# A hybrid decoder layer: DMA issues of recurrence and attention in source order, rotary products behind the exchange, low-rank chain begun later

## The chip, the cores and the metric

The kernel runs on 1 core of one Trainium2 chip. The metric is the device time of one execution in microseconds (us), lower is better. The core has five engines with their own instruction streams: TensorE (PE, matmul; its weight loads are shown as PEld), VectorE (DVE), ScalarE (ACT), GpSimd (POOL) and SyncE (SP). In this kernel SP issues all DMA transfers. Each engine takes its instructions strictly in the order of its stream, and an instruction that waits for a semaphore holds up those behind it.

## The reference, cut to what matters

One decoder layer on 1024 tokens of width 1024, all in float32. A gated merge of two mixers is followed by an MLP and a gated embedding:

```
u = rmsnorm(h);  z = u @ w_in
o_attn = dilated_attention(z_attn)        # 3 groups, (window, dilation) = (128,1), (512,4), (2048,16); 4 heads of 64 each
o_rwkv = rwkv7_time_mix(z_rwkv, ...)      # 8 heads of 64, a recurrence over the tokens
merged = sigmoid(z_gate_a) * (o_attn @ w_attn_up) + sigmoid(z_gate_r) * (o_rwkv @ w_rwkv_up)
h = h + rmsnorm(merged @ w_out)
h = h + rmsnorm(square(relu(rmsnorm(h) @ w_ff_in)) @ w_ff_out)
h = h + rmsnorm((p @ w_ple) * sigmoid(h @ w_ple_gate))
```

Queries and keys of the attention are rotated before the scores (rotary embedding): `rope(x) = [x1*cos - x2*sin, x2*cos + x1*sin]`, with x1 and x2 the two halves of a head. The recurrence needs a decay, a learning rate and a gate for each token and channel; these come from three low-rank products, for example `decay = exp(-exp(-softplus(-(w0 + tanh(xw) @ w2)) - 0.5))`.

## The kernel before

**Precision.** Every large product is made of three single-pass matmuls over high and low halves (`mm3`: high x high, high x low, low x high; lines 284, 286 and 288). A weight tile therefore needs two products before use: ACT writes the high half `wh`, POOL the low half `wl = wr - wh`.

**Stages.** First x is normalised and transposed into `uh` and `ul`, while the first two column tiles of z (inputs of the low-rank chain) are multiplied. Then come recurrence and attention, the part that the change touches. The output projection, the FFN and the embedding follow.

**Dense jobs.** The 46 further column tiles of z are dense jobs on PE: 12 for the recurrence (r, k, v for each of four pairs of heads, `add_rkv`), 18 for the attention (q, k, v for each of six pairs of heads, `add_attn`) and 16 for the gates (`add_gate`). A job has 2 halves of 24 matmuls. Each half is evacuated by ACT, and a gate's half is stored to DRAM (`gscr`). When a job begins, `fill` draws the next one and calls its `load`; `wload` (line 305) issues the DMA of 512 KB into one of two raw buffers `wr` and has the split on ACT and POOL emitted 3.9 us later in the plan (`soon(HOP_DMA + 1.4, split)`), or at the latest when that job begins. The very first job's split is therefore emitted as soon as it is drawn.

**Chains.** Everything else runs as Python generators beside the dense jobs: `lora_out` (the low-rank products, 24 stores to DRAM), `prepare` with `elementwise(w)` and `bonus(w)`, `inverses`, `rwkv` (`fold_v`, `fold`, `scan`, `read_out`, `post`) and `attention` (`turn`, `unit`). In `unit`, each block of 128 queries goes through scores on PE (`sc`), maximum on DVE (`SB`, `nm`), exponential on ACT, transposition on PE (`pt`), a copy on DVE (`PB`) and the product with V on PE (`po`).

**Who sets the order.** `Order` (line 131) is a planner that runs at build time. It keeps a modelled clock `t` for PE and an end for each engine, and lets each chain go on when its time has come; chains of lower priority number first, and a dense job's next matmul when no chain is due. The order in which instructions are emitted is the source order. Engines in a `manual_schedule` set keep this order: PE in the whole kernel (line 248), DVE, ACT and POOL from line 1167 to the end of `combine` (line 1161 leaves it). Before the change SP is in no such set: the framework's scheduler orders its DMA issues at build time by a model of its own, and may bring an issue forward as soon as its buffer and data are free. `spawn(gen, prio, after)` adds a chain that is first due `after` us from now. `HOP_DMA` is 2.5 us, the planner's price of a DMA from issue to landing. A POOL product is priced at 0.15 us and 0.0022 us for each element of a row.

**Rotary.** When the second half of a q or k tile `z` has been evacuated, four DMAs copy it with the halves of each head exchanged into `sw` (line 935). DVE multiplies `z` by the cosine in place (line 936). The chain `turned` (line 917) is due 2.7 us later: POOL multiplies `sw` by the sine, and after POOL's planned end DVE adds both.

**Elementwise and bonus.** `elementwise(w)` takes the tiles `En` and `a` (one buffer each) and loads the low-rank results into them. `bonus(w)` multiplies in the same buffer `a` and stores it to `bvscr`, after `elementwise(w)` has finished. Before the change, `elementwise(w + 1)` could take `a` in the source ahead of that store.

Of the kernel before, what the change touches and what calls it, by code (L numbers as in the profile page):

```python
# [13 lines left out]
OP = mybir.AluOpType  # L14
# [21 lines left out]
HOP, HOP_DMA = 0.15, 2.5  # L36
# [201 lines left out]
def layer(ctx: ExitStack, tc: tile.TileContext, x, pT, wz, wup, w_out, wff1, w_ff2, w_ple, w_pleg,  # L238
# [3 lines left out]
    sch = Order()  # L242
    SY = Loads(nc.sync, sch)
    V = Engine(nc.vector, sch, 0.18, 0.00104, True)
# [19 lines left out]
    done = set()  # L264

    def mm(out_, a, b, us, start=True, stop=True):
        PE.matmul(out_, a, b, start=start, stop=stop)  # L267
        m = math.prod(a.shape[1:])
        sch.turn("full" if a.shape[0] > 64 and m > 64 else (a.shape[0], m))
        sch.t = max(sch.t, sch.written.since(a, None) - 0.1, sch.written.since(b, None) - 0.1) + us  # L270
        sch.written.put(out_, sch.t, None)
        sch.dep = sch.t
# [8 lines left out]
    def mm3(ps, pairs):  # L281
        n = len(pairs)
        for i, (ah, al, bh, bl) in enumerate(pairs):
            PE.matmul(ps, ah, bh, start=i == 0, stop=False)  # L284
            yield MM
            PE.matmul(ps, ah, bl, start=False, stop=False)  # L286
            yield MM
            PE.matmul(ps, al, bh, start=False, stop=i == n - 1)  # L288
            yield MM

    def now(gen):
        for us in gen:
            sch.t += us
            sch.dep = sch.t

    def wait(cond):
        while not cond():
            yield 0.1

    def chain_bank(shape, name, tags=("m0", "m1")):  # L300
        tag = sch.first(tags)
        yield from sch.free(tag)
        return psum.tile(shape, F32, name=name, tag=tag), tag
# [134 lines left out]
    def rtile(shape, name, tag, dt=F32):  # L438
        n = 1
        for d in shape[1:]:  # L440
            n *= d
        assert n <= TAGN[tag], (shape, tag)
        return rt.tile(shape, dt, name=name, tag=tag, bufs=BUFS.get(tag, 1))
# [20 lines left out]
    def add_z(wi, evac, gate=None):  # L464
        def body(hi, lo):
            for h in range(2):
                ps = zbank()
                yield from zhalf(ps, hi, lo, h)
                evac(h, ps)
        sch.add(body, lambda: wload(wz[wi]), gate)  # L470
# [39 lines left out]
    def lora_out():  # L510
        S.activation(xw[0:96], xw[0:96], AF.Tanh)
        S.activation(xwh[0:96], xw[0:96], AF.Copy)
        V.tensor_tensor(xwh[32:64], xw[32:64], xwh[32:64], OP.subtract)
        S.activation(xg[0:96], xg[0:96], AF.Sigmoid)
        S.activation(xgh[0:96], xg[0:96], AF.Copy)
        V.tensor_tensor(xgl[0:96], xg[0:96], xgh[0:96], OP.subtract)
        S.activation(xa3[0:96], xar[0:96], AF.Copy)
        V.tensor_tensor(xa3[32:64], xar[32:64], xa3[32:64], OP.subtract)
        yield 9.0
        i = 0  # L520
        for w, n in [(w, n) for n in range(3) for w in range(NU)]:
            sl = slice(w * 128, w * 128 + 128)
            dst = (sa_scr[2 * w], sa_scr[2 * w + 1], og_scr[w])[n]
            for h in range(2):
                hs = slice(h * 512, h * 512 + 512)
                ps, tag = yield from chain_bank([128, 512], "lo", ("m0", "m1", "s1", "s2", "s3"))
                if n == 0:
                    mm(ps, wsh[0:96, sl], xwh[0:96, hs], MM)
                elif n == 1:
                    mm(ps, a2h[0:96, sl], xa3[0:96, hs], MM)  # L530
                else:
                    now(mm3(ps, [(g2r[0:96, 0, sl], g2r[0:96, 1, sl], xgh[0:96, hs], xgl[0:96, hs])]))
                st = lst[:, i % 8]
                i += 1
                if n < 2:
                    bc = (P_W0, P_A0)[n] + w
                    S.activation(st, ps, AF.Sigmoid, bias=pr[:, bc:bc + 1])
                else:
                    S.activation(st, ps, AF.Copy)
                sch.hold(tag)  # L540
                SY.dma_start(dst[:, hs], st)
                yield 0.6
            done.add(("lo", n, w))
# [32 lines left out]
    XY = {}  # L576

    def elementwise(w):
        yield from wait(lambda: ("lo", 1, w) in done)
        pc = lambda c: pr[:, c + w:c + w + 1]  # L580
        En = rtile([128, T], "En", "En")
        Ep = rtile([128, T], "Ep", "Ep")
# [292 lines left out]
    def prepare():  # L875
        for w in range(NU):
            yield from wait(lambda: w < 2 or ("F", w - 2) in done)
            yield from elementwise(w)
# [8 lines left out]
    def rwkv():  # L887
        for w in range(NU):
            yield from fold_v(w)
            yield from wait(lambda: ("T", w) in done)  # L890
            yield from fold(w)
            yield from scan(w)
            yield from read_out(w)
# [3 lines left out]
    rope_t, MD, NAT = {}, {}, {}  # L897

    def attn_ok(n, x):
        if n < 2:  # L900
            return (("S", NU - 2) in done and ("E", NU - 1) in done and ("bv", NU - 1) in done
                    and (x < 2 or n == 0 or ("vk", 0) in done and ("v", NU - 1) in done))
        return ("B", n - 2) in done and (x < 2 or ("vk", n - 1) in done)

    def add_attn(n):
        gi, hp = n // 2, n % 2
        g = GORD[gi]
        d = DILS[g]
        L = T // d
        base = 14 + (g * 2 + hp) * 3  # L910
        A[n] = {}

        def permuted(dst, ps, h):
            S.activation(dst.rearrange("p (r i) -> p i r", r=d)[:, h * (L // 2):(h + 1) * (L // 2), :],
                         ps.rearrange("p (i r) -> p i r", r=d), AF.Copy)

        def turned(z, sw):
            G.tensor_tensor(sw, sw, rope_t[g][:, 1], OP.mult)
            yield sch.until(G.end)
            V.tensor_tensor(z, z, sw, OP.add)  # L920
            A[n].setdefault("qk", []).append(V.end)

        def qk(x):
            def evac(h, ps):
                if h == 0:
                    A[n][x] = rtile([128, T], "qk", (("r", "Ep"), ("k", "En"))[x][hp])
                    if g not in rope_t:
                        rope_t[g] = rtile([128, 2, T], "rope", f"AR{gi % 2}")
                        SY.dma_start(rope_t[g], rope[g].rearrange("a p t -> p a t"))
                z = A[n][x]  # L930
                permuted(z, ps, h)
                if h == 1:
                    sw = rtile([128, T], "sw", ("a", "kk")[x])
                    for b in range(4):
                        SY.dma_start(sw[32 * b:32 * b + 32], z[32 * (b ^ 1):32 * (b ^ 1) + 32])
                    V.tensor_tensor(z, z, rope_t[g][:, 0], OP.mult)
                    sch.spawn(turned(z, sw), 1, HOP_DMA + 0.2)
            return evac

        def v_evac(h, ps):  # L940
            if h == 0:
                A[n]["vx"] = rtile([128, T], "v", "v" if n else "TM0")
            permuted(A[n]["vx"], ps, h)
            if h == 1:
                A[n][2] = A[n]["vx"]
                A[n]["t"] = sch.dep
        for x, evac in enumerate((qk(0), qk(1), v_evac)):
            add_z(base + x, evac, lambda x=x: attn_ok(n, x))
# [159 lines left out]
    def combine(OT, OA, stat, sel):  # L1108
# [56 lines left out]
    sch.t = V.end = S.end = G.end = 0.0  # L1165
    sch.written = Written()
    in_turn = tc.manual_schedule(
        engines={mybir.EngineType.DVE, mybir.EngineType.Activation, mybir.EngineType.Pool})
    in_turn.__enter__()
    sch.spawn(lora_out(), 2)  # L1170
    sch.spawn(rwkv(), 0)
    sch.spawn(inverses(), 1)
    sch.spawn(prepare(), 1)
# [590 lines left out]
```

## Time and profile before

| | us |
|---|---|
| median of 3 runs (lowest, highest) | 1889.44 (1887.34, 1893.47) |
| the profiled execution | 1891.43 |
| its span, from first to last instruction | 1889.6 |

The trace's mean granted TensorE clock is 0.972. The rows of the profile have the forms "line engine operation out<-in". A helper records every ACT, DVE and POOL operation, so all of them have line 115, and all DMA issues of the planned part line 128; they are told apart by their tiles. `z<-uh,wh` is a dense job's matmul, `wh<-wr` and `wl<-wr,wh` its weight's split, `wr<-in_wz_dram` its load. `sw<-qk` is the rotary exchange, `qk<-qk,rope` the cosine product, `sw<-sw,rope` the sine product, `qk<-qk,sw` the sum. A timeline row begins with start and duration in us; in brackets behind it stand the idle time of the engine before it and what ended that. Waits are listed with their total in us, how often they occurred, and the longest. SPq is SP's queue. A DMA row ends with the median time from issue to landing.

### The profile page before, as it was taken

What the parts mean: (1) busy time and instruction counts of PE and PEld (TensorE: products, weight loads), DVE (VectorE), ACT (ScalarE), POOL (GpSimd) and SP (SyncE); (2) the same over time, 40 slices, a digit from 0 to 9 for tenths busy, and PEclk for the clock granted to TensorE, in tenths of its full rate; (3) what the DMA queues carried; (4) which work ended last, traced back from release to release, by engine and by line L of the source; (5) the groups of instructions that cost most, each with busy time, mean ns of one, the idle gap of its engine ahead of it and who ended that gap; (6) DMA issues with size and microseconds to landing.
All of it is one profiled execution on the core that took longest, in us unless ns stands there. A gap on an engine that the chain in (4) does not pass through costs nothing.

```text
span 1889.6 us, 25877 instructions
## 1 busy us (share of the span) xinstructions
PE 1791.9 (95%) x10192; PEld 1448.6 (77%) x10192; DVE 1079.0 (57%) x1866; ACT 728.1 (39%) x1301; POOL 773.4 (41%) x507
## 2 busy tenths in 40 slices
PE   8899999999997999988999999999999999999898
PEld 8687877777775676766788878888888888887787
DVE  6268875666534343334473646555555677788444
ACT  5633433341313343235252544333333333334354
POOL 1344221231122122222223046666666797896411
PEclk9899999999899999999899999999999999999999
DMA  4522112212222122123352411111111211112311
GB/s 161 186 94 67 46 63 73 79 46 84 74 89 73 67 57 56 45 67 114 109 211 87 162 51 63 60 45 45 56 45 45 68 55 45 45 56 71 108 67 56
DMA packets 51546, 146.13 MB, mean 77 GB/s; under 512 B 6241, under 2 KB 6625, under 8 KB 51426
## 3 DMA queue, kind: packets, MB, share of 16 engines
q1 hardware_dynamic: 51426, 144.49, 23.3%
q8 instruction: 80, 1.31, 0.3%
q14 instruction: 40, 0.33, 0.1%
HBM read 110.52 MB, written 27.26 MB: 73 GB/s over the span
## 4 chain that ended last, share of the span: by engine, by line
PE 80%; DVE 9%; ACT 3%; issue 3%; DMA 2%; POOL 1%; SPq 1%; DVEq 0%; POOLq 0%; ACTq 0%
PE z L288 16%; PE z L284 16%; PE z L286 16%; PE bk L284 6%; PE bk L288 6%; PE bk L286 6%; DVE xy L115 1%; DVE pt L115 1%; DMA sw<-qk 1%; DVE tot L115 1%; DVE yc L115 1%; PE sc L267 1%; PE tp L275 1%; PE y L267 1%; SPq L128 1%
## 5 line engine op out<-in xcount | busy, mean ns | idle before, releaser
L115 DVE TENSOR_TENSOR tot<-tot,bk 128x512 f32<-128x512 f32 x468 | 308.2, 685 | 189.8 <-PE bk L288 189.1
L115 POOL TENSOR_TENSOR wl<-wr,wh 128x1024 fp32r<-128x1024 f32 (+1 forms) x88 | 214.4, 2437 | 397.6 <-ACT wh L115 380.5
L284 PE MATMUL z<-uh,wh 128*128 128x512 f32 (+1 forms) x800 | 325.4, 407 | 15.5 <-ACT wh L115 8.1
L288 PE MATMUL z<-uh,wl 128*128 128x512 f32 (+1 forms) x800 | 325.2, 406 | 9.1 <-POOL wl L115 8.9
L286 PE MATMUL z<-ul,wh 128*128 128x512 f32 (+1 forms) x800 | 324.5, 406 | 0.3 <-DVE ul L115 0.3
L284 PE MATMUL z<-f,wh 128*128 128x512 f32 x512 | 199.9, 390 | 1.9 <-ACT f L115 1.9
L286 PE MATMUL z<-f,wh 128*128 128x512 f32 x512 | 200.0, 391 | 0.2 <-DVE f L115 0.2
L288 PE MATMUL z<-f,wl 128*128 128x512 f32 x512 | 199.7, 390 | 0.0
L284 PEld LDWEIGHTS z<-uh,wh 128*128 128x128 f32 x800 | 156.3, 195 | 49.9 <-ACT wh L115 8.3
L288 PEld LDWEIGHTS z<-uh,wl 128*128 128x128 f32 x800 | 156.6, 196 | 43.7 <-POOL wl L115 11.5
L286 PEld LDWEIGHTS z<-ul,wh 128*128 128x128 f32 x800 | 156.4, 196 | 34.1 <-issue 6.5
L115 ACT ACTIVATE duo<-sum 128x512 fp32r<-128x512 f32 x150 | 90.3, 625 | 226.3 <-PE bk L288 113.0
L284 PE MATMUL bk<-duo 128*128 128x512 f32 x420 | 163.4, 389 | 0.0
L286 PE MATMUL bk<-duo 128*128 128x512 f32 x420 | 163.4, 389 | 0.0
L288 PE MATMUL bk<-duo 128*128 128x512 f32 x420 | 163.4, 389 | 0.0
L115 POOL TENSOR_TENSOR duo<-sum,duo 128x512 fp32r<-128x512 f32 x75 | 100.7, 1343 | 102.2 <-ACT duo L115 102.2
L115 ACT ACTIVATE wh<-wr 128x1024 fp32r<-128x1024 f32 (+1 forms) x88 | 91.1, 1036 | 59.9 <-PE z L286 51.7
L284 PEld LDWEIGHTS z<-f,wh 128*128 128x128 f32 x512 | 96.4, 188 | 22.2 <-ACT f L115 2.1
L286 PEld LDWEIGHTS z<-f,wh 128*128 128x128 f32 x512 | 96.5, 188 | 20.5 <-DVE f L115 0.5
L288 PEld LDWEIGHTS z<-f,wl 128*128 128x128 f32 x512 | 96.5, 189 | 20.0
L115 POOL TENSOR_TENSOR sw<-sw,rope 128x1024 f32<-128x1024 f32 x12 | 39.9, 3328 | 175.4 <-DMA sw<-qk 153.6
L115 POOL TENSOR_TENSOR sum<-w2r 128x512 f32<-128x512 f32 x75 | 98.8, 1317 | 21.8 <-DVE yc L115 17.1
(302 smaller groups left out, 3295.7 us busy)
## 6 DMA issues: line engine op xcount, KB each, us to landing
wr<-in_wz_dram SPq DMA_DIRECT2D x48, 512.0 KB, 3.5
w2r<-in_w_ff_dram SPq DMA_DIRECT2D x32, 512.0 KB, 3.6
wr<-in_wff_dram SPq DMA_DIRECT2D x32, 512.0 KB, 3.5
xt<-in_x_dram SPq DMA_DIRECT2D x16, 512.0 KB, 4.4
gscr<-gst SPq DMA_DIRECT2D x32, 256.0 KB, 2.0
g<-gscr SPq DMA_DIRECT2D x16, 512.0 KB, 4.1
sw<-qk SPq DMA_DIRECT2D x48, 128.0 KB, 2.3
sascr<-lst SPq DMA_DIRECT2D x16, 256.0 KB, 2.9
```

The costliest lines, as they stand in the source:

```text
L115: return f(*a, **kw)
L128: return self.eng.dma_start(out_, in_)
L267: PE.matmul(out_, a, b, start=start, stop=stop)
L275: PE.transpose(out_, a, ident if idn is None else idn)
L284: PE.matmul(ps, ah, bh, start=i == 0, stop=False)
L286: PE.matmul(ps, ah, bl, start=False, stop=False)
L288: PE.matmul(ps, al, bh, start=False, stop=i == n - 1)
```

## The change

Four edits, all in recurrence and attention:

- SP joins the engines that keep the source order.
- `elementwise(w)` waits until `bonus(w - 1)` has issued its store.
- The cosine product moves from the evacuation into `turned`, behind the sine product in the source, and `turned` is due 4.9 us instead of 2.7 us after the evacuation.
- `lora_out` is first due at 0.3 us of the plan instead of 0.

```
     def elementwise(w):
-        yield from wait(lambda: ("lo", 1, w) in done)
+        yield from wait(lambda: ("lo", 1, w) in done and (w == 0 or ("bv", w - 1) in done))
...
         def turned(z, sw):
             G.tensor_tensor(sw, sw, rope_t[g][:, 1], OP.mult)
+            V.tensor_tensor(z, z, rope_t[g][:, 0], OP.mult)
             yield sch.until(G.end)
             V.tensor_tensor(z, z, sw, OP.add)
...
                         SY.dma_start(sw[32 * b:32 * b + 32], z[32 * (b ^ 1):32 * (b ^ 1) + 32])
-                    V.tensor_tensor(z, z, rope_t[g][:, 0], OP.mult)
-                    sch.spawn(turned(z, sw), 1, HOP_DMA + 0.2)
+                    sch.spawn(turned(z, sw), 1, HOP_DMA + 2.4)
...
     in_turn = tc.manual_schedule(
-        engines={mybir.EngineType.DVE, mybir.EngineType.Activation, mybir.EngineType.Pool})
+        engines={mybir.EngineType.DVE, mybir.EngineType.Activation, mybir.EngineType.Pool, mybir.EngineType.SP})
     in_turn.__enter__()
-    sch.spawn(lora_out(), 2)
+    sch.spawn(lora_out(), 2, 0.3)
```

More of the change, by code (lines that the diff above doesn't have):

```diff
@@ L578, in elementwise @@
     def elementwise(w):
-        yield from wait(lambda: ("lo", 1, w) in done)
+        yield from wait(lambda: ("lo", 1, w) in done and (w == 0 or ("bv", w - 1) in done))
         pc = lambda c: pr[:, c + w:c + w + 1]
@@ L918, in turned @@
             G.tensor_tensor(sw, sw, rope_t[g][:, 1], OP.mult)
+            V.tensor_tensor(z, z, rope_t[g][:, 0], OP.mult)
             yield sch.until(G.end)
@@ L935, in evac @@
                         SY.dma_start(sw[32 * b:32 * b + 32], z[32 * (b ^ 1):32 * (b ^ 1) + 32])
-                    V.tensor_tensor(z, z, rope_t[g][:, 0], OP.mult)
-                    sch.spawn(turned(z, sw), 1, HOP_DMA + 0.2)
+                    sch.spawn(turned(z, sw), 1, HOP_DMA + 2.4)
             return evac
@@ L1167, in layer @@
     in_turn = tc.manual_schedule(
-        engines={mybir.EngineType.DVE, mybir.EngineType.Activation, mybir.EngineType.Pool})
+        engines={mybir.EngineType.DVE, mybir.EngineType.Activation, mybir.EngineType.Pool, mybir.EngineType.SP})
     in_turn.__enter__()
-    sch.spawn(lora_out(), 2)
+    sch.spawn(lora_out(), 2, 0.3)
     sch.spawn(rwkv(), 0)
```

## Prediction

> **What bounds the kernel now.** I read the page first, then the table by stage, then PE's waits, then the timeline around the longest of them.
>
> ```profile
> PE 1791.9 (95%) x10192; PEld 1448.6 (77%) x10192; DVE 1079.0 (57%) x1866; ACT 728.1 (39%) x1301; POOL 773.4 (41%) x507
> 520.00:870.00 350.00, 310.72 (x1833) 234.12 (x1830) 132.92 (x341) 122.21 (x277) 89.31 (x33) 0.95 0.23 68
> ```
>
> The second row gives the stretch and its length, then busy time and count of PE, weight loads, DVE, ACT and POOL, the granted clock, and the DMA share. TensorE is the bound, and the change leaves its instructions as they are. All the time there is to win is TensorE's idle time and its half-clock time inside the recurrence and attention, which end near 930 us; the FFN behind them is not touched. In the attention stretch PE is idle for 350.00 - 310.72 = 39 us. PE's waits from 40 to 930 us, each with total, times and longest:
>
> ```profile
> PE po L267 <- DVE PB L115: 25.3, 10, 6.1
> PE z L288 <- POOL wl L115: 8.9, 4, 5.4
> PE z L284 <- ACT wh L115: 8.1, 1, 8.1
> ```
>
> These three are what the change can reach: P copies late on DVE, and weight splits late on POOL and ACT. Long idle also costs clock. These stretches were taken around the half-clock periods:
>
> ```profile
> 53.00:60.20 7.20, 5.60 (x12) 3.96 (x13) 0.55 (x1) 0.89 (x1) 5.07 (x2) 0.50 0.34 101
> 592.00:600.00 8.00, 7.47 (x30) 5.27 (x31) 4.04 (x16) 4.75 (x17) 2.35 (x1) 0.57 0.22 66
> 613.00:620.00 7.00, 5.13 (x17) 3.39 (x18) 4.77 (x4) 1.09 (x1) 3.69 (x2) 0.51 0.62 212
> 715.50:722.30 6.80, 6.42 (x23) 4.46 (x24) 4.29 (x3) 1.11 (x1) 4.53 (x2) 0.50 0.15 36
> 770.00:773.50 3.50, 3.50 (x18) 2.35 (x15) 2.10 (x3) 1.09 (x1) 3.04 (x2) 0.52 0.02 5
> 824.00:828.00 4.00, 4.00 (x17) 2.98 (x17) 3.24 (x1) 0.60 (x1) 3.06 (x2) 0.59 0.00 0
> 851.00:856.00 5.00, 3.79 (x15) 3.03 (x15) 2.24 (x1) 0.99 (x2) 1.16 (x1) 0.66 0.55 180
> ```
>
> Length times (1 - clock) is the work lost. The five rows from 592 to 828 give 3.4 + 3.4 + 3.4 + 1.7 + 1.6 = 13.5 us. They stand behind P waits, so those waits cost at most 25.3 + 13.5 = 38.8 us. The last row costs 5.00 x 0.34 = 1.7 us.
>
> **Low-rank chain 0.3 us later.** Both chain and first weight tile are planned at time 0, and today the chain goes first, so ACT does its tanh, sigmoid and copies ahead of the first weight split:
>
> ```profile
> 42.02 0.69 ACT L115 ACTIVATE xw<-z,omu 128x512 f32<-128x512 f32 x1 [3.84 <-PE z L288]
> 51.91 1.99 ACT L115 ACTIVATE wh<-wr 128x1024 fp32r<-128x1024 f32 x2
> 53.02 5.07 POOL L115 TENSOR_TENSOR wl<-wr,wh 128x1024 fp32r<-128x1024 f32 x2 [34.07 <-ACT wh L115]
> 44.58 0.28 PE L288 MATMUL z<-uh,wl 128*128 128x256 f32 x1
> 53.00 0.79 PE L284 MATMUL z<-uh,wh 128*128 128x512 f32 x1 [8.14 <-ACT wh L115]
> 55.82 0.79 PE L288 MATMUL z<-uh,wl 128*128 128x512 f32 x1 [1.60 <-POOL wl L115]
> 60.20 0.40 PE L284 MATMUL z<-uh,wh 128*128 128x512 f32 x1
> 60.44 0.40 PE L286 MATMUL z<-ul,wh 128*128 128x512 f32 x1
> ```
>
> PE ends the input stage at 44.9 and gets its third matmul of the first tile (the first that needs the low half) only at 55.82. It then runs at half clock; the matmul at 60.20 is the thirteenth (12 in the row 53.00:60.20). With 0.3 us of delay the planner draws the first tile before the chain and issues its split at once. ACT is free from 42.02 + 0.69 = 42.7, so the high half is done at 43.7 (1.99 / 2), the low half at 46.3 (5.07 / 2), and the third matmul can start there. Ten steps of 0.24 us, from the last two rows, put the thirteenth at 48.7 instead of 60.2: 11.5 us. If ACT first evacuates the last input half (PE is through at 44.9), everything is 2.7 us later, and with a half clock behind that gap another 1.9 us go: 6.9 us is the low end. I take 10.5, nearer to the first, since the split needs only weights. The chain starts about 1 us later; its first products are planned 9 us on, with the 48 matmuls of the first tile (11.5 us) as cover. Without that cover the 1 us would show.
>
> **Rotary cosine product behind the exchange.** One q or k tile, on ACT, SP, DVE, POOL and PE in turn:
>
> ```profile
> 708.88 1.07 ACT L115 ACTIVATE qk<-z 128x512 f32<-128x512 f32 x1 [0.92 <-PE z L288]
> 709.74 1.07 ACT L115 ACTIVATE wh<-wr 128x1024 fp32r<-128x1024 f32 x1
> 709.98 2.42 SPq L128 DMA_DIRECT2D sw<-qk  x4
> 714.26 1.22 DVE L115 TENSOR_TENSOR qk<-qk,rope 128x1024 f32<-128x1024 f32 x1 [6.51 <-DMA sw<-qk]
> 715.41 1.01 DVE L115 COPY PB<-pt 128x256 f32<-128x256 f32 x2
> 717.74 3.37 DVE L115 TENSOR_TENSOR qk<-qk,sw 128x1024 f32<-128x1024 f32 x1 [1.31 <-POOL sw L115]
> 714.30 3.40 POOL L115 TENSOR_TENSOR sw<-sw,rope 128x1024 f32<-128x1024 f32 x1 [18.00 <-DMA sw<-qk]
> 717.66 2.37 POOL L115 TENSOR_TENSOR wl<-wr,wh 128x1024 fp32r<-128x1024 f32 x1
> 715.88 0.69 PE L267 MATMUL po<-PB,vkb 128*64 128x128 f32 x4 [3.52 <-DVE PB L115]
> DVE qk L115 <- DMA sw<-qk: 104.1, 12, 18.3
> ```
>
> The cosine product overwrites what the exchange DMAs read, so it waits for them, and on the in-order DVE the two P copies behind it wait too. That makes PE's 3.52 us gap. It happens 12 times and blocks DVE for 104.1 us in all, not all of it with work behind. The exchange lands 714.26 - 708.85 = 5.4 us after the z tile; the new planned delay is 2.5 + 2.4 = 4.9 us. So P copies planned before that pass, and some 0.5 us of waiting remains. The product itself is only moved.
>
> What is late next is POOL. At 4.9 us the sine product comes behind the weight split, planned at 3.9 us. Price for this tile: the planner adds 2.40 us for each POOL product (0.15 + 1024 x 0.0022), so it places DVE's final sum at 10.35 us, that is at 719.2.
>
> **DMA issues in source order.** Today loads run ahead of their place, as soon as a raw buffer is free:
>
> ```profile
> SPq L128 <- POOL wl L115: 720.9, 86, 27.2
> 720.06 0.33 SPq L128 DMA_DIRECT2D wr<-in_wz_dram  x1
> wr<-in_wz_dram SPq DMA_DIRECT2D x48, 512.0 KB, 3.5
> ```
>
> Held to the source, the next tile's load stands behind the four exchange DMAs: issued at 709.98 + 2.42 = 712.4, landed 3.5 us later at 715.9. Its split is planned at 708.85 + 3.9 = 712.75, so ACT sits 3.2 us with exponentials queued behind it. The high half ends at 717.0, the low half 2.37 later at 719.4, before today's 720.0, so PE does not miss it. The sine product then runs to 722.8 at 3.40, and DVE waits 722.8 - 719.2 = 3.6 us at the sum with P copies behind it.
>
> So per tile a DVE block of 6.51 + 1.22 + 1.31 = 9.0 us becomes one of 0.5 + 1.2 + 3.6 = 5.3 us, on other copies, and ACT gains one of 3.2 us. Of 38.8 us I take half as won, 19 us: above the 41% by which the DVE block shrinks, because the clock needs long gaps to fall. Of ACT's 12 x 3.2 = 38 us I let one eighth, 5 us, reach PE, because mostly no exponentials are planned just behind. Attention: -14 us, between -38.8 (all won, nothing paid) and +20 (below).
>
> The clock term has a row and a rule that differ:
>
> ```profile
> 768.87 0.44 PE L267 MATMUL po<-PB,vkb 128*64 128x128 f32 x4 [2.96 <-DVE PB L115]
> ```
>
> A 2.96 us gap was followed by the half clock of the row 770.00:773.50, so I let shorter leftover gaps keep half of the 13.5 us. The Trainium skill ("TensorE: Matmul & The Clock Gate", Why this matters for your kernels) advises against idle gaps over about 3 us; by that limit leftover gaps would cost no clock and the sum would be 6.7 us lower. This row is just under it and the clock fell, so the trace decides.
>
> The other way round, a load can no longer hold up an exchange:
>
> ```profile
> 836.73 0.59 ACT L115 ACTIVATE qk<-z 128x512 f32<-128x512 f32 x1
> 839.35 0.33 SPq L128 DMA_DIRECT2D wr<-in_wz_dram  x1
> 839.73 2.42 SPq L128 DMA_DIRECT2D sw<-qk  x4
> ```
>
> The tile was ready at 837.3 and its exchange left 2.4 us later; 5.4 us of waiting for the low half plus 1.7 us of clock followed at 852. I count 4 of these 7.1 us (bounds 0 and 7.1).
>
> The 16 gate jobs have the store of their last half ahead of the next load. Evacuation (0.59, as in the row 836.73), 0.33 of issue and 3.5 of landing come to 4.4 us, 0.5 behind the planned 3.9: 8 us of ACT waiting, of which I put half on PE, +4; bounds 0 and 8.
>
> **The wait for the bonus store.** The elementwise step may not take buffer `a` before the store that reads it has been issued. SP's later loads and stores queue behind these DMAs.
>
> ```profile
> 129.83 0.32 SPq L128 DMA_DIRECT2D bvscr<-a  x1
> 132.42 0.32 SPq L128 DMA_DIRECT2D a<-sascr  x1
> 149.01 1.15 ACT L115 ACTIVATE kk<-k,pr 128x1024 f32<-128x1024 f32 x1 [1.20 <-POOL k L115]
> ```
>
> The load already follows the store, and its consumer's step begins at 149.01 with k, 17 us later. So 0; without k's tile as cover it would be the 2.6 us between the two issues, three times: 0 to 8.
>
> **Sum.** -10.5 - 14 - 4 + 4 + 0 = -24.5 us. The profiled execution took 1891.4 us around its span of 1889.6, the runs' median is 1889.4. I put the sum to the median: 1865.
>
> **Rivals.**
> 1. *Everything pays.* All P waits go, and the 852 us gap too: 1889.4 - 11.5 - 38.8 - 7.1 = 1832. For it: every half-clock row of attention is behind a P wait. Against: the 3.4 us sine product now last on POOL.
> 2. *The start alone.* New DVE and ACT waits eat all of attention: 1889.4 - 10.5 = 1879. For it: the tile above, where the DVE block only shrinks.
> 3. *Weights come late (slower).* Place: ACT's wait for a raw tile. Each of 12 rotary tiles shows its 3.2 us on PE and the half clock behind it, 1.7 us: 59 us against 38.8 won, +20; the gate jobs pay their 8. 1889.4 - 10.5 + 20 + 8 = 1907. It decides once 49 of these 67 us show on PE (38.8 + 10.5 are won), so when in three tiles of four ACT has planned work within 3.2 us of a split. Against: today only 8.9 us of PE waits stand on the low half. The Trainium skill ("DMA: Bandwidth & Descriptors", Anatomy of one DMA) says that a DMA's semaphore wait happens on the issuing sequencer, before dispatch; by that rule every load behind a waiting store slips as here. The trace agrees at 839.35, where the exchange queued behind a load left 2.4 us late.
> 4. *Nothing much.* The scheduler's issue order was nearly the source's, the split stays behind the chain on ACT, and POOL takes over DVE's stall: 1889, within the noise.
>
> **How the numbers follow.** Forecast 0.45 (1853 to 1876), everything pays 0.17, start alone 0.16, weights late 0.14, nothing 0.08. A measurement of this kernel can tell about 0.3%, 5.7 us. Faster: 0.45 + 0.17 + 0.16 = 0.78; same 0.08; slower 0.14. The range from 1840 to 1897 leaves out about half of rival 1 and most of rival 3, 2 in 10.
>
> **What would show it.** Right: the first z wait on ACT near 45 us falls from 8.1 to under 2 and the 53 to 60 us half clock is gone; DVE's waits for the exchange fall from 104 to some 10 to 30 us, and part of it reappears as waits for POOL's sine product, some 40 us; the P waits halve; ACT shows new waits for raw weight tiles, about 40 us, and SP's waits for POOL's low half (720.9) go. Wrong: P waits still near 25 us, z waits on ACT or POOL above 20 us in all, or a start that still has the chain ahead of the split.

## The result and the profile after

| | before | after |
|---|---|---|
| median of 4 runs each, us | 1891.45 (1887.34 to 1900.31) | 1845.62 (1843.28 to 1850.24) |
| the profiled execution, us | 1891.43 | 1844.24 |
| its span, us | 1889.6 | 1842.1 |
| mean granted TensorE clock | 0.972 | 0.984 |

The kernel after takes 0.9755 of the time before, 95% interval 0.9713 to 0.9796: 45.8 us less by the medians, 47.5 us less in the span. From the page of the kernel after, part 1:

```profile
PE 1773.0 (96%) x10192; PEld 1436.4 (78%) x10192; DVE 1063.7 (58%) x1866; ACT 729.2 (40%) x1301; POOL 760.9 (41%) x507
```

The counts are those of before. PE's busy time fell by 18.9 us (1791.9 before) although it does the same matmuls: that is half-clock time gone. In the timeline of the kernel before, dense matmuls start 0.43 us apart at clock 0.50 (57.26, 57.69) and 0.23 us apart at full clock (61.38, 61.61), and the half-clock time up to 930 us fell from 85 to 38 us. The other 28.6 us of the span were idle time.

Where they were won: the table by stage, cut at the first rotary exchange and at the last product with V. Columns as in the prediction: window, length, busy time and count of PE, weight loads, DVE, ACT, POOL, granted clock, DMA. Of the kernel before:

```profile
44.60:519.30 474.70, 442.79 (x3642) 359.81 (x3642) 300.89 (x527) 180.79 (x268) 124.63 (x93) 0.96 0.25 82
519.30:882.10 362.80, 323.52 (x1939) 243.18 (x1934) 138.76 (x358) 127.14 (x291) 91.69 (x34) 0.95 0.22 66
```

Of the kernel after:

```profile
44.60:500.20 455.60, 432.73 (x3592) 352.19 (x3591) 297.81 (x527) 176.64 (x260) 122.65 (x93) 0.98 0.24 81
500.20:822.50 322.30, 303.85 (x1938) 229.17 (x1936) 124.22 (x360) 129.36 (x297) 74.76 (x32) 0.99 0.25 76
```

Attention has the same number of matmuls (1939 and 1938) and is 40.5 us shorter. Its idle time fell from 362.80 - 323.52 = 39.3 to 322.30 - 303.85 = 18.4 us, its clock rose from 0.95 to 0.99. The recurrence lost 9.0 us of idle time (31.9 to 22.9) and went from 0.96 to 0.98. It also has 50 matmuls fewer, which come later, so its 19.1 us are not all a gain.

The waits from 40 to 930 us (total, times, longest). Of the kernel before, the one row that the prediction did not need:

```profile
DVE qk L115 <- POOL sw L115: 13.7, 7, 2.3
```

Of the kernel after:

```profile
PE po L267 <- DVE PB L115: 6.8, 8, 1.5
PE sc L267 <- DVE qk L115: 5.8, 5, 1.3
PE z L288 <- POOL wl L115: 2.8, 4, 1.4
ACT wh L115 <- DMA wr<-in_wz_dram: 102.6, 26, 6.9
DVE qk L115 <- POOL sw L115: 63.0, 11, 6.9
DVE qk L115 <- DMA sw<-qk: 37.5, 11, 9.4
```

PE's waits for P copies fell from 25.3 to 6.8 us, and no longer exceed 1.5 us. Yet DVE stands still almost as long as before at the rotary tiles: 37.5 + 63.0 = 100.5 us, against 104.1 + 13.7 = 117.8. And ACT has 102.6 us of new waits for raw weight tiles. New on PE are five waits of scores for the rotated tile, 5.8 us.

The start of the recurrence, from the timeline of the kernel after:

```profile
41.94 1.06 ACT L115 ACTIVATE wh<-wr 128x1024 fp32r<-128x1024 f32 x1 [3.77 <-issue]
42.91 0.67 ACT L115 ACTIVATE xw<-z,omu 128x512 f32<-128x512 f32 x1
45.54 0.50 PE L288 MATMUL z<-uh,wl 128*128 128x512 f32 x1 [0.21 <-POOL wl L115]
47.92 0.39 PE L284 MATMUL z<-uh,wh 128*128 128x512 f32 x1
```

The split now goes ahead of the last evacuation `xw`; the third matmul waits 0.21 us, and the thirteenth stands at 47.92 instead of 60.20: 12.3 us won.

One rotary tile of the kernel after (timeline, same columns):

```profile
667.77 1.07 ACT L115 ACTIVATE qk<-z 128x512 f32<-128x512 f32 x1 [0.92 <-PE z L288]
668.87 2.42 SPq L128 DMA_DIRECT2D sw<-qk  x4
671.40 0.52 SPq L128 DMA_DIRECT2D wr<-in_wz_dram  x1
673.12 1.22 DVE L115 TENSOR_TENSOR qk<-qk,rope 128x1024 f32<-128x1024 f32 x1 [2.53 <-DMA sw<-qk]
675.12 1.06 ACT L115 ACTIVATE wh<-wr 128x1024 fp32r<-128x1024 f32 x1 [2.24 <-DMA wr<-in_wz_dram]
676.25 2.40 POOL L115 TENSOR_TENSOR wl<-wr,wh 128x1024 fp32r<-128x1024 f32 x1 [21.05 <-ACT wh L115]
678.61 2.39 POOL L115 TENSOR_TENSOR sw<-sw,rope 128x1024 f32<-128x1024 f32 x1
681.03 1.23 DVE L115 TENSOR_TENSOR qk<-qk,sw 128x1024 f32<-128x1024 f32 x1 [6.69 <-POOL sw L115]
```

This is the sequence that the prediction drew: the load behind the four exchange DMAs, ACT waiting for it, the low half done 678.65 - 668.84 = 9.8 us after the tile (10.6 forecast), the sine product behind it, DVE standing at the sum. Both waits on DVE are longer than forecast, 2.53 us at the exchange (0.5) and 6.69 at the sum (3.6), so DVE's block in this tile is 2.53 + 1.22 + 6.69 = 10.4 us, not the 5.3 of the forecast, and longer than the 9.0 of before. ACT's wait is shorter, 2.24 us (3.2).

### The profile page after: what moved, and what is told of

Its sections match the earlier page's. It is cut to its first block, busy times and chain, and to the rows that moved or that the text cites. A ratio compares the mean times of both kernels' runs of the same rounds, so it can differ in the third digit from the quotient of the medians.

```text
span 1842.1 us, 25869 instructions
## 1 busy us (share of the span) xinstructions
PE 1773.0 (96%) x10192; PEld 1436.4 (78%) x10192; DVE 1063.7 (58%) x1866; ACT 729.2 (40%) x1301; POOL 760.9 (41%) x507
## 4 chain that ended last, share of the span: by engine, by line
PE 53%; DVE 2%; ACT 1%; DMA 0%; POOL 0%; issue 0%; DVEq 0%; POOLq 0%; ACTq 0%
PE z L288 11%; PE z L286 11%; PE z L284 11%; PE bk L284 6%; PE bk L286 6%; PE bk L288 6%; DVE tot L115 1%; PE tp L275 1%; PE cb L267 0%; PE po L267 0%; DMA wr<-in_w_pleg_dram 0%; PE sc L267 0%; DMA wr<-oscr 0%; PE pt L275 0%; POOL wpg L115 0%
## 5 line engine op out<-in xcount | busy, mean ns | idle before, releaser
L284 PE MATMUL z<-uh,wh 128*128 128x512 f32 (+1 forms) x800 | 320.6, 401 | 6.2 <-ACT part L115 3.3
L288 PE MATMUL z<-uh,wl 128*128 128x512 f32 (+1 forms) x800 | 319.1, 399 | 2.8 <-POOL wl L115 2.8
L286 PE MATMUL z<-ul,wh 128*128 128x512 f32 (+1 forms) x800 | 319.2, 399 | 0.3 <-DVE ul L115 0.3
L286 PEld LDWEIGHTS z<-f,wh 128*128 128x128 f32 x512 | 96.5, 189 | 20.4 <-DVE f L115 0.4
L115 POOL TENSOR_TENSOR sum<-hr 128x512 f32<-128x512 f32 x75 | 97.5, 1309 | 4.8 <-DVE duo L115 3.1
```

Source lines behind the costliest of these rows:

```text
L115: return f(*a, **kw)
```

## The experiments

Each kernel was compared with the kernel before on the same chip. "Start" is the low-rank chain at 0.3 us, "rotary" the cosine product behind the exchange with the delay of 2.4, "SP" the source order for SP's DMAs with the wait for the bonus store.

| run | what it has | median us | against before, us | ratio, 95% interval |
|---|---|---|---|---|
| e1_lora | start alone | 1880.74 | -10.4 | 0.9925 to 0.9960 |
| e2_rot | rotary alone | 1849.48 | -41.6 | 0.9753 to 0.9816 |
| e3_sp | SP alone | 1872.15 | -18.9 | 0.9873 to 0.9941 |
| e4_nosp | start and rotary | 1836.40 | -54.7 | 0.9685 to 0.9752 |
| after | all | 1845.62 | -45.8 | 0.9713 to 0.9796 |
| e5_split_late | after, all splits 3 us later | 1844.37 | -45.3 | 0.9704 to 0.9788 |
| e6_turn_late | after, rotary chain 4 us later | 1837.12 | -52.5 | 0.9677 to 0.9755 |
| e7_rot_move_only | rotary's move alone | 1867.82 | -21.8 | 0.9838 to 0.9911 |
| e8_rot_delay_only | rotary's delay alone | 1881.42 | -8.2 | 0.9919 to 0.9965 |
| e9_sp_recurrence | after, SP free in attention | 1836.87 | -53.7 | 0.9704 to 0.9731 |
| e10_split_behind_exchange | after, 12 splits 3 us later | 1837.56 | -53.0 | 0.9708 to 0.9735 |
| e11_split_and_turn | e10, rotary chain 1 us later | 1835.26 | -55.3 | 0.9696 to 0.9723 |
| e12_free_sp_turn_late | SP free in all stages, rotary chain 4 us later | 1835.59 | -55.0 | 0.9677 to 0.9709 |

**The parts.** The wait for the bonus store was not run by itself. Two of the runs, e4 without it and e9 with it, have the same order of instructions on PE, DVE, ACT and POOL, and their times are 0.5 us apart.

The start alone:

```
-    sch.spawn(lora_out(), 2)
+    sch.spawn(lora_out(), 2, 0.3)
```

> The kernel before with one edit: the low-rank chain due at 0.3 us of the plan. Theory (the parts add up: 12 us at the start, about 35 us in attention from the moved cosine product, next to nothing from the issue order): the first z wait on ACT of 8.1 us and the half clock from 50 to 60 us go, 12 us less, about 1879 against 1891. Rival A (the issue order of SP carries the attention gain): the same here. Rival B (the start is won but given back later, since the chains end when they did): within 4 us of before.

Measured: -10.4 us. From its timeline:

```profile
45.51 0.50 PE L288 MATMUL z<-uh,wl 128*128 128x512 f32 x1 [0.21 <-POOL wl L115]
```

The start is that of the kernel after, so this edit makes it by itself, and of the 12.3 us that it wins there 10.4 are left at the end: rival B falls. In this run the P waits fell as well, from 25.3 to 17.8 us, although the rotary products are where they were; PE's idle time in attention stayed at 39.2 us. The total of one kind of wait moves with any shift of the plan, so it has to be read together with the idle time of its stage.

Rotary alone (the two hunks of `turned` and `qk` in the diff, nothing else):

> The kernel before with the cosine product moved into the chain and that chain due 4.9 us instead of 2.7 us after the evacuation; SP stays with the scheduler. Theory: P waits on PE fall from 25 to below 10 us and the half clock behind them goes, 30 to 35 us less, about 1858. Rival A: the P waits stay near 20 us, at most 8 us less, about 1884.

Measured: -41.6 us. Its waits:

```profile
PE po L267 <- DVE PB L115: 5.7, 6, 1.5
```

The P waits go with this edit and without any change of SP's order. Rival A, in which they stay near 20 us, falls; the gain is larger than the theory's 30 to 35 us.

SP alone (SP in the ordered set, and the wait for the bonus store):

> The kernel before with SP in source order and the wait for the bonus store that this order needs. Theory: between 10 us less and 5 us more; ACT waits about 100 us for raw weight tiles and PE hardly shows it, P waits stay near 25 us. Rival A: 25 us less or better, P waits halve. Rival C (late weights cost): 10 us more or worse, with z waits of PE on ACT or POOL above 15 us.

Measured: -18.9 us, outside what the theory allowed (-10 to +5). PE and DVE have the same order of instructions as before here, so only times differ. Its waits:

```profile
PE po L267 <- DVE PB L115: 22.8, 10, 4.0
PE z L288 <- POOL wl L115: 2.0, 2, 1.6
```

Its attention stage:

```profile
508.80:863.80 355.00, 323.46 (x1940) 243.31 (x1935) 136.27 (x358) 120.51 (x284) 88.17 (x33) 0.95 0.23 68
```

Two things make it up. In attention 7.7 us of idle time are gone (355.00 - 323.46 = 31.5, before 39.3). The waits for the low half fell by about as much (8.9 to 2.0), with them the 5.4 us behind the exchange that a load held up at 839. The other 10.5 us are in the recurrence, whose stretch is 508.8 - 44.6 = 464.2 instead of 474.7 us long with only 1.5 us less of idle time: nearly all of it is clock. The half-clock time in this stretch fell from 37.5 to 17.1 us. The largest piece of the difference, 10.2 us that begin at 503.9 in the kernel before, stands behind a window with 2.18 us of 32x32 matmuls (last section). A smaller piece shows how little decides: in both kernels PE waits 3.26 us for ACT until 164.4. The windows of the kernel before:

```profile
162.52:165.93 3.41, 1.50 (x6) 1.24 (x7) 2.64 (x3) 3.41 (x6) 3.41 (x2) 1.00 0.01 2
165.93:169.34 3.41, 3.41 (x10) 2.63 (x9) 3.38 (x4) 0.55 (x1) 3.41 (x5) 0.50 0.00 0
```

And of the kernel with SP alone:

```profile
162.54:165.95 3.41, 1.53 (x7) 1.27 (x8) 2.67 (x3) 3.41 (x6) 3.41 (x2) 1.00 0.01 2
165.95:169.37 3.42, 3.42 (x17) 2.84 (x16) 3.39 (x4) 0.53 (x1) 3.42 (x5) 1.00 0.00 0
```

PE was idle for 1.91 and for 1.88 us of the first window; the clock fell to 0.50 behind the one and stayed at 1.00 behind the other. The last section comes back to this. No step of the edit was found that would explain these clock gains; they may be no more than the accident of where a gap falls.

Start and rotary, the change without SP's order:

```
-        engines={... mybir.EngineType.Pool, mybir.EngineType.SP})
+        engines={... mybir.EngineType.Pool})
```

> The changed kernel with SP given back to the scheduler (and without the wait for the bonus store): low-rank chain later and cosine product moved. Theory: the two gains add, 40 to 47 us less than before, about 1848, the changed kernel's time within 5 us. Rival A: about 1879, some 33 us above the changed kernel.

Measured: 1836.4 us, 9.2 under the kernel after (6.6 in the spans of the profiled executions), which neither the theory nor the rival had. PE and DVE have the order of the kernel after. So the gains of start and rotary add up (-52.0 as a sum, -54.7 together), and SP's order, worth -18.9 us alone, costs 9 beside them: what it wins alone (the held-up exchange) the rotary edit has removed already (the low half costs PE 1.6 us in the run with rotary alone). Its gain in clock is not there either: the recurrence has 20.5 us at half clock with SP's order and without.

**What SP's order costs.** The attention stage of the run with start and rotary, to be read beside that of the kernel after:

```profile
501.10:816.90 315.80, 304.19 (x1938) 230.31 (x1935) 124.40 (x360) 126.90 (x294) 88.56 (x33) 0.98 0.25 73
```

DVE's waits for the sine product in it:

```profile
DVE qk L115 <- POOL sw L115: 22.9, 8, 4.6
```

Attention has 11.6 us of idle time instead of 18.4, DVE stands 22.9 us at the sums instead of 63.0, and no score waits for a rotated tile (5.8 us in the kernel after). Without SP's order the load has run ahead, the low half is done when the exchange lands, and the sine product follows at once. The next runs test whether this is the cause. All splits 3 us later, so that the sine product goes first:

```
-            sch.soon(HOP_DMA + 1.4, split)
+            sch.soon(HOP_DMA + 4.4, split)
```

> The kernel after, with each weight split put into ACT's and POOL's order 3.0 us later (6.9 instead of 3.9 us after its load). The question is what SP's source order costs beside the two other edits: 1845.6 us with it, 1836.4 without, with the same order of instructions on PE and DVE. Theory (the weight splits come too early for the late loads): ACT's 102.6 us of waits for raw tiles are what the 9 us are; with the later split they fall below 40 us, the sine product goes ahead of the low half on POOL, DVE's waits for POOL's sine product fall from 63 to some 25 us, and the time is 1836 to 1841. Rival A (the low half is then late for its matmuls): PE's waits for the low half grow from 2.8 to over 15 us, time 1855 or more. Rival B (the 9 us are half-clock time that comes and goes with any shift): ACT's waits fall, the time stays at 1843 to 1849.

Measured: 1844.4 us, the time of rival B, but the waits of the theory, and some of rival A's:

```profile
ACT wh L115 <- DMA wr<-in_wz_dram: 30.4, 14, 5.2
DVE qk L115 <- POOL sw L115: 20.3, 10, 2.3
PE z L288 <- POOL wl L115: 11.4, 7, 3.5
```

Its recurrence and its attention stage:

```profile
44.60:508.60 464.00, 439.77 (x3594) 358.54 (x3594) 293.15 (x527) 177.60 (x261) 123.84 (x93) 0.96 0.24 80
508.60:823.60 315.00, 305.45 (x1932) 230.52 (x1930) 135.50 (x360) 126.94 (x292) 87.46 (x32) 0.98 0.26 77
```

The windows decide: attention is 7.3 us shorter than in the kernel after, the recurrence, where no exchange stands ahead of a load, 8.4 us longer at 0.96 instead of 0.98. There PE now waits 10.6 of the 11.4 us for late low halves, rival A's mechanism; the idle time of the recurrence grew by only 1.3 us, its half-clock time from 20.5 to 37.5 us. Two effects cancel; the run alone settles nothing.

SP in source order up to the first exchange only, then free (a second ordered set for SP alone, left at the first exchange):

```
                 if h == 1:
+                    if sp_turn:
+                        sp_turn.pop().__exit__(None, None, None)
                     sw = rtile(...)
```

> The kernel after, with SP held to the source order in the recurrence only: from the first rotary exchange on, SP's DMAs are free again. The order on PE, DVE, ACT and POOL is that of the kernel after, but for the few places where ACT and POOL are free again behind the planned part. Theory (the 9 us that SP's order costs beside the other edits arise in attention, where each load stands behind four exchange DMAs, so that the low half goes ahead of the late sine product on POOL): 1834 to 1838, DVE's waits for POOL's sine product fall from 63 to some 25 us. Rival (they arise in the recurrence): 1843 to 1848.

Measured: 1836.9 us (1835.94 to 1838.37); no run of the kernel after is below 1843.28. What SP's order costs arises in attention: the spans of the two profiled executions differ by 5.5 us, their attention stages by 5.9. Its attention stage:

```profile
500.90:817.30 316.40, 304.77 (x1938) 230.60 (x1936) 124.47 (x360) 126.92 (x294) 88.56 (x33) 0.98 0.25 73
```

The recurrence (44.6 to 500.9) is as long as in the kernel after, attention has 11.6 us of idle time, and DVE's waits for the sine product are 22.9 us, as with SP free throughout. The other way to the same end is SP in source order throughout, with only the 12 splits whose load stands behind an exchange 3 us later:

```
-            sch.soon(HOP_DMA + 1.4, split)
+            sch.soon(HOP_DMA + (4.4 if behind else 1.4), split)
+            behind.clear()
...
+                    behind.append(n)
                     sch.spawn(turned(z, sw), 1, HOP_DMA + 2.4)
```

> The kernel after, with only those weight splits put 3.0 us later whose load stands behind a rotary exchange (the run with every split later won 10 us in attention and lost them in the recurrence: its time was that of the kernel after). Theory: recurrence as in the kernel after, attention as in that run, so 1833 to 1838, ACT's waits for raw tiles below 60 us, DVE's for the sine product near 20 us. Rival (the later low half costs PE what the earlier sine wins): 1842 to 1848.

Measured: 1837.6 us. Its waits:

```profile
ACT wh L115 <- DMA wr<-in_wz_dram: 63.0, 25, 5.1
DVE qk L115 <- POOL sw L115: 20.3, 10, 2.3
```

With SP's order kept and the sine product ahead of the low half, 8 of the 9 us come back, while ACT still waits 63 us (below 60 was expected). PE's idle time in attention is 12.8 us, against 18.4 in the kernel after and 11.6 with SP free, and no score waits for a rotated tile. So most of what SP's order costs comes with the late sine product. What ACT's waits cost by themselves is not separated by this run, since they fell too; that it is little is suggested by the run with the rotary chain 4 us later (below), where 117.8 us of them stand beside 14.4 us of idle time in attention.

**The rotary edit in halves.** The move without the delay (`turned` due at `HOP_DMA + 0.2` as before, the cosine product in it):

> The kernel before, with the cosine product moved into the rotary chain, but the chain still due 2.7 us after the evacuation. Both halves of the rotary edit together gave -42 us. Theory: what counts is that DVE's stalling instruction is planned after the exchange lands (5.4 us), so the move to 2.7 us wins about half of the block of 6.5 us per tile: -15 to -25 us, PE's waits for P copies fall from 25.3 to some 15 us. Rival A (the move is all, since the delay only adds a wait for the sine product): -35 to -45. Rival B (the delay is all): -8 to 0.

The delay without the move (`HOP_DMA + 2.4`, the cosine product left at the evacuation):

> The kernel before, with the rotary chain due 4.9 instead of 2.7 us after the evacuation, and the cosine product left at the evacuation. Theory: DVE stands at the cosine product as long as before (104 us of waits for the exchange), so the time stays within 6 us of before: 1885 to 1894, PE's waits for P copies 20 to 27 us. Rival (the delay is all): DVE's sum comes late enough, -20 us or more.

Measured: -21.8 and -8.2 us. Waits of the run with the move:

```profile
PE po L267 <- DVE PB L115: 8.9, 8, 2.4
PE z L288 <- POOL wl L115: 8.6, 3, 6.6
```

Of the run with the delay:

```profile
PE po L267 <- DVE PB L115: 22.7, 10, 4.1
DVE qk L115 <- DMA sw<-qk: 101.2, 12, 16.1
PE z L288 <- POOL wl L115: 1.6, 1, 1.6
```

The move takes most of the P waits (8.9 left, some 15 expected) and leaves the late low half; the delay does little for the P waits, as expected, but ends the wait for the low half (8.9 to 1.6 us), which fits a time 3.6 us below the theory's band. Together they give -41.6, more than the -30 of their sum.

**Rotary chain later.** In the kernel after 4 us later (`HOP_DMA + 6.4`), the order on POOL unchanged:

> The kernel after, with the rotary chain (sine, cosine, sum) due 8.9 instead of 4.9 us after the evacuation; POOL's order stays the same, so only the place of cosine and sum on DVE moves. Theory of the weight splits: the loads are as late as before, but DVE no longer stands at the sum; if DVE's 100 us of waits for exchange and sine are what PE still pays, the time falls to 1838 to 1842 and DVE's waits for both fall below 40 us. Rival: PE waits for DVE's P copies are only 6.8 us in the kernel after, so there is nothing left to win there: 1843 to 1849.

Measured: 1837.1 us, just below the theory's band, but not for its reason: DVE's waits hardly fell (28.8 us for the exchange, and for the sine product the row below).

```profile
DVE qk L115 <- POOL sw L115: 61.1, 10, 6.9
```

From its timeline, the first product that spreads the attention's row sums (`row`) behind the last P copies:

```profile
832.40 1.10 PE L267 MATMUL cb<-row,sel 64*128 64x512 f32 x3 [1.82 <-DVE row L115]
```

The same in the timeline of the kernel after:

```profile
839.54 1.65 PE L267 MATMUL cb<-row,sel 64*128 64x512 f32 x3 [5.00 <-DVE row L115]
```

And the window behind it, of the kernel after:

```profile
838.60:852.30 13.70, 12.76 (x25) 7.83 (x26) 7.99 (x13) 3.14 (x5) 4.88 (x3) 0.50 0.18 58
```

In the kernel after a 5.00 us gap stands there, and 13.70 us at clock 0.50 begin with it. With the later chain the gap is 1.82 us and no half clock follows. Some 3 us of gap and 6.9 of clock (13.70 x 0.50) go there; the whole stretch behind the last product with V is 5.8 us shorter (1019.6 to 1013.8). That is about half of the 10.6 us between the two spans. The other half is in attention, 322.3 to 316.9 us long, where PE's idle time fell from 18.4 to 14.4 us and the waits of scores for the rotated tile from 5.8 to 2.8. The runs e4 and e9 have the same 13.7 us at half clock at this place, so it is no part of what SP's order costs. Why DVE's row sums come earlier there was not tried.

The rotary chain 1 us later on top of the 12 later splits (`HOP_DMA + 3.4`), and 4 us later with SP free in all stages:

> The same, and the rotary chain due 5.9 instead of 4.9 us after the evacuation, behind the exchange's landing (5.4 us) and still ahead of the split (6.9 us). Theory: DVE stands some 12 x 0.5 us less at the exchange, 0 to 3 us under the run with the later splits alone. Rival: the sine product is later too and slips behind the low half on POOL; DVE's waits for it return to 60 us, and the time to 1838 to 1846.

> The kernel after with SP's DMAs free in all stages (1836.4 us in an earlier run) and the rotary chain due 8.9 instead of 4.9 us after the evacuation (1837.1 in an earlier run with SP held to the source order). Theory (two ways to take DVE's stall out of the way of the P copies; they overlap): 1832 to 1837. Rival A (they add up): 1826 to 1831. Rival B (the sums, now later, hold up the scores of the next head): 1837 to 1845, and PE's waits for the rotated q and k above 8 us.

Measured: 1835.3 and 1835.6 us (1832.79 to 1839.06, 1828.46 to 1836.43). Both lie in the bands of their theories, and with the free SP and the 12 later splits they make four versions between 1835.3 and 1837.6 us, not to be told apart by these runs, that beat the kernel after by 8 to 10 us. The ways to take DVE's stall aside do not add up.

## Why the prediction came out as it did

The time, 1845.6, lies within the range (1840 to 1897), and the order of events was right. The forecast of 1865 gave a gain of 24.5 us, little more than half of the 45.8 that were measured, and the time is only 5.6 us above the lower end of the range. Point by point:

1. **Start**: -10.5 forecast, -12.3 in the trace (its working allowed 11.5; the split goes even ahead of the last evacuation), -10.4 by the run with this edit alone. Right.
2. **Attention, the term that was mis-sized.** The step read: "Of 38.8 us I take half as won, 19 us: above the 41% by which the DVE block shrinks". The P waits fell from 25.3 to 6.8 us, and the five half-clock rows behind them (13.5 us) are gone; the one half-clock row left in attention, at 555, stands behind a wait for ACT (`yt <- rb`, 3.1 us). So 18.5 + 13.5 = 32 of 38.8 us were won. Two assumptions failed. First, that PE's waits shrink as DVE's do. DVE's block was to shrink by 41%; its waits at the rotary tiles shrank from 117.8 to 100.5 us, by 15%, the P waits to about a quarter. Two errors met here: the block stayed nearly as long, and its length was not what PE pays for. What counts is what is queued behind the wait. The prediction's own remark, "P copies planned before that pass", says so, but it was not carried into the size. In the kernel before, P copies stood directly behind a waiting cosine product in 4 of 12 tiles. From its timeline two of them (the others are the tile at 714 of the prediction and one at 767), and as the last line one more long P wait:

```profile
611.07 3.41 DVE L115 TENSOR_TENSOR qk<-qk,rope 128x1024 f32<-128x1024 f32 x1 [5.59 <-DMA sw<-qk]
614.40 0.74 DVE L115 COPY PB<-pt 128x256 f32<-128x256 f32 x2
614.87 0.69 PE L267 MATMUL po<-PB,vkb 128*64 128x128 f32 x4 [6.06 <-DVE PB L115]
821.28 1.23 DVE L115 TENSOR_TENSOR qk<-qk,rope 128x1024 f32<-128x1024 f32 x1 [5.51 <-DMA sw<-qk]
822.43 1.28 DVE L115 COPY PB<-pt 128x512 f32<-128x512 f32 x2
823.16 0.66 PE L267 MATMUL po<-PB,vkb 128*64 128x128 f32 x8 [3.37 <-DVE PB L115]
592.52 0.65 PE L267 MATMUL po<-PB,vkb 128*64 128x128 f32 x4 [4.50 <-DVE PB L115]
```

   With the 2.96 us at 768.87 and the 3.52 at 715.88 these four gaps make 15.9 of the 25.3 us, and four of the five half-clock rows (613, 715, 770, 824) belong to them. The fifth row, 592, belongs to the last line above: there DVE waits 6.34 us at the cosine product of 588.08 with a maximum of scores (`SB`) directly behind it and the P copy 4 us later. Together these five make 20.4 us. In the kernel after, the P copies of such a unit are ahead of the cosine product (670 in the tile above, cosine at 673), and the long waits at the sum (6.69 us) have no copy behind them: the next one comes 7 us or more after the sum in all but one of the tiles. Second, the step on the clock kept half of the 13.5 us for shorter gaps; the P waits that were left, of at most 1.5 us, brought none.
3. **ACT's waits.** Forecast 38 us at the rotary tiles and 8 at the gates, of which one eighth, 5 us, would reach PE. ACT waits 102.6 us in all, more than twice the 46. The toll on PE is 7 us of idle time in attention, 9 by the medians. The size was near, by luck, since the path was another: not exponentials behind a waiting split, but the sine product behind the late low half, and scores waiting for the sum (5.8 us). The prediction had that late sine product too, but charged it to DVE's block. The runs with the 12 later splits and with SP free in attention show it.
4. **An exchange no longer held up**: -4 forecast; PE's waits for the low half fell from 8.9 to 2.8 us, -6. Right in size, but it did not need SP's order: SP alone brings it to 2.0 us, rotary alone and even the delay alone to 1.6.
5. **Gate jobs**: +4 forecast; the waits for the low half, 2.8 us in the whole stretch, leave no room for it. **Bonus store**: 0, as forecast.

Terms 1 to 5 as measured, -12 - 32 + 7 - 6, make -43 of the 47.5 us in the span. Two gains that no term had fit the rest. In the kernel before, the waiting cosine product of 545.11 also held up an instruction of the recurrence (`AR`), and PE's gap of 3.63 us at 546.58 and 3.4 us at half clock went with it; the kernel after has no such wait in attention. And the half-clock time of the recurrence behind the start fell from 27.3 to 20.5 us. Longer waits elsewhere take some of this back (`yt <- rb` 8.7 us instead of 5.5, `cb <- row` 5.0 instead of 3.3).

The rivals: "everything pays" (1832) was nearer than the forecast; without SP's order the kernel comes within 5 us of it. "Weights come late" had its mechanism, waits for raw tiles, at more than the forecast size, but its condition failed: 49 us would have had to show on PE, and 7 to 9 did. Of the signs named, the first z wait, the half clock at 53 to 60, and SP's waits for the low half came as named (between 40 and 930 us they fell from 342.0 to 24.7 us; the 720.9 of the prediction count the whole span); DVE's waits for exchange and sine (37.5 and 63.0) exceeded their bands (10 to 30, some 40), ACT's for raw tiles theirs too (102.6, about 40), and the P waits fell to a quarter, not to half.

## What to carry to other kernels

Price a wait on an in-order engine by the instructions directly behind it, one place after another, not by its total: here 118 us of standing still cost PE 25 to 39 us, and 100 us cost 7. When an instruction that waits for a DMA is moved behind the DMA's landing, look also at what else on that engine and on the next one is now ahead of it; a step that only enforces the source order can undo part of that by making loads late. Test the parts alone and without one another: one that wins 19 us alone cost 9 in company.

## What the runs showed of the hardware

**The clock is decided in fixed windows.** In all fourteen traces the half-clock periods that begin between 44 and 940 us begin on one grid of 3.4133 us, to within 0.01 us, and last one to four steps of it. Cut along this grid from 45 to 930 us, with PE's idle time counted in each window that was at full clock: all 106 windows with more than 1.9 us of idle time were followed by half clock, 16 of 105 between 1.0 and 1.9, and 7 of 3175 below 1.0. So not the length of a gap alone decides but how it lies: the 3.26 us gap at 164 fell into two windows, and the second, with about 1.9 us idle (1.91 and 1.88 in the windows shown), was followed by half clock in the kernel before and not in the kernel with SP alone. This is no sharp threshold: in the kernel before a window with 1.75 us was followed (544.83) and one with 1.88 was not (541.42). The 2.96 us gap at 768 cost 3.41 us at half clock. The Trainium skill ("TensorE: Matmul & The Clock Gate", What's actually happening) gives a free-running window of 3413 ns; the traces agree with that length. It puts the fall behind an idle window; here a window a little more than half idle was enough. By these counts the P waits of at most 1.5 us that are left rarely cost clock, so the clock term of the prediction was set too high.

**Small matmuls.** Idle time does not explain the seven windows below 1.0 us. Each of them holds 1.2 to 2.4 us of 32x32 matmuls (`tq` or `tr`, from the inverses); in the kernel before, the window from 500.46 to 503.87 has 0.48 us of idle time and 2.18 us of them, and 10.2 us at half clock follow. They do not decide it alone: of the 102 windows with more than 1.0 us of them and less than 1.9 us idle, 8 were followed by half clock. What they do to the clock was not tried.

**Loads in source order.** The median time from issue to landing of a 512 KB weight tile rose from 3.5 to 4.3 us with SP in source order. The exchange is not the only cause: in the kernel after, the eleven loads whose landing can be told and that stand directly behind an exchange took 3.8 us in the median, the eleven behind the store of a gate 4.2 and the nine behind another weight load 4.6. At the rotary tile shown above, the load leaves 2.5 us behind the first exchange DMA (668.87, 671.40), and ACT waits 2.24 us for it.
